# Dilated attention of a two-block network: strided values projected feature-major, scores over 64 partitions in two banks

## The chip, the cores and the metric

The kernel runs on one core of one Trainium2 chip. The metric is device time in microseconds (us) of one launch, the median of several runs. A profiled execution is one more launch, of which the hardware profiler kept every instruction; all rows below are from such an execution.

## The reference, cut to what matters

Two network blocks on 1024 tokens of 1024 features follow each other. The second block normalises its input, projects it with one matrix and feeds four mixers, of which dilated attention is one. It has twelve heads of 64 features in three groups of four. A group has a window and a dilation (128 and 1, 512 and 4, 2048 and 16). The tokens of a group are taken apart by the dilation, and each query attends to the keys of its own and the previous band:

```
def dilated_group(q, k, v, bias_tab, window, dil):
    ...
    qb = to_sub(q).reshape(B_, dil, H, nb, band, E)
    kb = band_keys(to_sub(k))
    vb = band_keys(to_sub(v))
    ...
    s = jnp.einsum('bdhnqe,bdhnke->bdhnqk', qb, kb, preferred_element_type=jnp.float32) / math.sqrt(E)
    s = jnp.where(mask[None, None, None], s + bias[None, None, :, None], -1e30)
    m = jnp.max(s, axis=-1, keepdims=True)
    p = jnp.exp(s - m)
    den = jnp.sum(p, axis=-1, keepdims=True)
    o = jnp.einsum('bdhnqk,bdhnke->bdhnqe', p, vb.astype(jnp.float32)) / den
    lse = (m + jnp.log(den))[..., 0]
    ...
```

The three groups' outputs are then weighted by a softmax over their `lse`.

## The kernel before

`build` runs the first block, then `stick`, `dilated`, `s5` (with the pooling mixer) and the merge of the second block. Everything is written by hand against one core; a scheduler sets the order of each engine's instructions at build time, and that order is then fixed. Activations lie feature-major: eight tiles of 128 features by 1024 tokens, each in a high and a low f32r part (`xh`, `xl`), so that a product is three products (high by high, low by high, high by low).

`gemm` (L357, L359, L361) makes a feature-major projection: 128 output features, 8 feature tiles, two halves of 512 tokens, three products, so 48 matmuls with 512 moving columns, where a weight tile is stationary. Its weights come through `load_w` (L325), which loads 512 KB and splits it on ACT (L381) and DVE (L382). `tm_gemm` (L1581 to L1583) makes a token-major projection instead: 128 tokens of x are stationary, 256 columns of weights move, 24 matmuls for a block of 128 tokens.

`dilated` goes through three groups g with dilations 1, 4 and 8 (the third group's 16 is handled as 8 with every second distance masked). For each group:

- a bias tile per head (L1733), made from a small table;
- values V (L1743 to L1752): 8 blocks of 128 tokens by `tm_gemm`, where `nat` picks each block's tokens, so that for g of 1 and 2 the stationary operand is every 4th or 8th column of x; ACT copies each result to `vd` (L1751);
- queries and keys by `gemm`, m from 0 to 3: ACT writes q (`dq`, L1761), with the tokens put into strided order on the way; each k is written twice into tiles of 128 partitions that POOL has set to zero (`dk`, L1767), head 0 of a pair by DVE into partitions 0 to 63 (L1772), head 1 by ACT into 64 to 127 (L1770), so that a product over 128 partitions takes one head alone;
- 8 blocks n of 128 queries: scores of the four heads (L1790), with 128 or 256 keys, two heads of a pair side by side in one PSUM bank; bias and maximum on DVE (L1793), exponential on ACT (L1798), transposes on TensorE (L1803), copies `dpt` to SBUF (L1806, L1808), products with V (L1815), copies of the result to `num` (L1818, L1820).

Ahead of group 0's blocks and behind every second block `fill` puts one gate projection of the later merge (`gate`, another `gemm` of 48 matmuls), which the scheduler lays between the block's own steps. At the end the groups are weighted: two more gates, then 24 products over 32 partitions (L1883). Two PSUM places of 1024 columns (`pmm`, tiles `mm`) and four banks (`pax`, tiles `ax`) are shared by all of this.

Of the kernel before, what the change touches and what calls it, by code (L numbers as in the profile page):

```python
# [30 lines left out]
# pieces of the down-projection, those by plain products, and when a piece's parts are made:  # L31
# counted in products before the next piece, and around those of a pair of rows
# [7 lines left out]
# ---------------------------------------------------------------- host layout  # L40
# [98 lines left out]
def layout(i):  # L139
# [58 lines left out]
    A["w_dv"] = np.stack([np.ascontiguousarray(wd[:, 2, g]).reshape(KC, P, 256) for g in range(3)])  # L198
# [53 lines left out]
# ---------------------------------------------------------------- device code  # L252


class Kern:
# [26 lines left out]
    # two places, in turn unless the caller says which  # L282
# [15 lines left out]
    # one gate of the merge, to keep the tensor engine busy meanwhile  # L298
# [25 lines left out]
    # weights of one output tile, split into two f32r parts  # L324
# [11 lines left out]
    # up to four weight tiles, split  # L336
# [11 lines left out]
    # out[128 features, tokens] for each (psum AP, list of hi APs, list of lo APs)  # L348
# [14 lines left out]
    # activations are lists of feature tiles for each half of the tokens  # L363
# [6 lines left out]
    # slots that hold two feature tiles of one half  # L370
# [17 lines left out]
    # y = v^-1/2 for a small tile v, by Newton steps from an integer guess  # L388
# [15 lines left out]
    # running sum of (g x)^2 over the feature tiles  # L404
# [9 lines left out]
    # sums over partitions, token-major [128, blocks]  # L414
# [8 lines left out]
    # token-major [128, blocks] to a row that all partitions hold  # L423
# [23 lines left out]
    # rows r1 = rstd(x) and r1 * rstd(x r1 g), from the sums of x^2 and (g x)^2  # L447
# [15 lines left out]
    # (x * rstd) * g + s, split  # L463
# [18 lines left out]
    # ------------------------------------------------------------ adaptive modulation  # L482
# [21 lines left out]
    # ------------------------------------------------------------ first block, mixing half  # L504
    def block1_mix(self):
# [18 lines left out]
        # the stages of a normed tile: times rstd, scaled, shifted, split  # L524
# [104 lines left out]
        # output gates, queries of both mixers  # L629
# [37 lines left out]
        # the context  # L667
# [50 lines left out]
        # token-major projections: values and gates  # L718
# [37 lines left out]
        # keys and queries of the recurrent heads, the other modulation columns in between  # L756
# [27 lines left out]
        # the last recurrent head comes last  # L784
# [10 lines left out]
        # output projection onto the residual, with the norm that follows  # L795
# [12 lines left out]
    # last products of a residual, a half of the tokens at a time, each half's norm under the next products;  # L808
    # the residual goes to DRAM, the normed activations B become the seven right factors of the
    # 2 x 2 product of Strassen and Winograd (rows: halves of the features, columns: halves of the tokens)  # L810
# [30 lines left out]
    # T1 = B12 - B11, T3 = B22 - B12, T2 = T3 + B11, -T4 = B21 - T2, the last three in the place of x  # L841
# [37 lines left out]
    # one row of the up-projection's tiles a and v, by seven products instead of eight:  # L879
    # a = A11 B1 + A12 B2, v = A21 B1 + A22 B2 over the halves of the features  # L880
# [49 lines left out]
    # gated hidden units to DRAM; the first two pairs side by side while the factors are formed  # L930
    def up(self, fp, W, B, steps, act):
# [11 lines left out]
        for j in range(2, NF):  # L943
            # the last product of a pair behind the first one of the next
            new = run(j)
            next(new)
            next(cur)
            for _ in range(5):
                next(new)
            cur = new  # L950
# [3 lines left out]
    # hidden units back on chip in pieces, times the down-projection onto the residual, by seven  # L954
    # products over the halves of features and tokens; the last piece is left to the caller,
    # for the norm that follows
    def down(self, fp, W, xd, yd, add):
# [5 lines left out]
        # the right factors of a piece, in the order of the products  # L963
# [53 lines left out]
        # both parts of the first and the last piece  # L1017
# [17 lines left out]
        # rows m and m + 4 of the output: what is done when, counted in products  # L1035
        def pair(m, j0, pn, B):
# [21 lines left out]
            # S3 in the place of A11, S4 in that of A21  # L1058
# [68 lines left out]
    # recurrent heads and window attention side by side  # L1127
# [13 lines left out]
    def window(self, ep, qd, kd, kcd, va):  # L1141
        nc, A = self.nc, self.A
        ID = self.c("ident")
        # keys of a group twice along the partitions, for queries that hold both parts of their split
# [14 lines left out]
        # the queries of a unit, high parts over low parts  # L1159
# [17 lines left out]
        # shifted exponentials of the scores, over their sum  # L1177
# [40 lines left out]
        def values(n, v, ss, rd):  # L1218
# [22 lines left out]
            if v:  # L1241
                # over the sums of the exponentials, as rows
# [23 lines left out]
    # depthwise convolution of three taps along the tokens of a PSUM tile  # L1266
# [6 lines left out]
    def mlstm(self, ep, km, kc, qm, vx, so, G):  # L1273
# [6 lines left out]
        # log sigmoid of the forget gates  # L1280
# [37 lines left out]
        # in token order, and token-major copies  # L1318
# [26 lines left out]
        for h in range(4):  # L1345
# [4 lines left out]
            # states at the chunk starts  # L1350
# [46 lines left out]
            # decay from key to query and from the chunk start to the query  # L1397
# [34 lines left out]
            # outputs of both directions  # L1432
# [30 lines left out]
            # norm over the head's features, gain and output gate  # L1463
# [20 lines left out]
    # ------------------------------------------------------------ first block, feed-forward half  # L1484
# [30 lines left out]
    # ------------------------------------------------------------ second block  # L1515
    # both norms between the blocks, under the last products of the first block
    def block2_norm(self, xs, out):
# [14 lines left out]
        # queries and keys of the first head, first half of the tokens  # L1532
# [30 lines left out]
    # token-major projection of 128-token blocks: out[tokens, columns]  # L1563
# [26 lines left out]
    # ------------------------------------------------------------ stick-breaking attention  # L1590
    def stick(self):
# [36 lines left out]
        with tc.tile_pool(name="sb", bufs=1) as fp:  # L1628
# [54 lines left out]
            for h in range(4):  # L1683
# [3 lines left out]
                # the next head's projections, or a gate, between the two halves of the queries  # L1687
# [13 lines left out]
    # ------------------------------------------------------------ dilated attention  # L1701
    def dilated(self):
# [3 lines left out]
        with tc.tile_pool(name="dl", bufs=1) as fp:  # L1706
# [10 lines left out]
            for g, dil in enumerate((1, 4, 8)):  # L1717
                # additive bias and mask of each head, Toeplitz in query and key
# [24 lines left out]
                wh, wl = self.tm_weights(A["w_dv"][g], 256)  # L1743
                vs = []
                for b in range(8):
                    if b % 4 == 0:
                        vt = self.big("vd")
                    ps = self.pax(256)
                    self.tm_gemm(ps, lambda x: nat(x, b), wh, wl)
                    v = vt[:, (b % 4) * 256 : (b % 4 + 1) * 256]  # L1750
                    nc.scalar.activation(v, ps, AF.Copy)  # L1751
                    vs.append(v)  # L1752
                q, k = [], []
                for m in range(4):
# [3 lines left out]
                    pv = ps.rearrange("p (l s) -> p l s", s=dil)  # L1758
                    if m < 2:
                        t = self.big("dq")  # L1760
                        nc.scalar.activation(t.rearrange("p (s l) -> p l s", s=dil), pv, AF.Copy, scale=0.125)  # L1761
                        q.append(t)
                    else:
                        kk = []
# [598 lines left out]
```

## Time and profile before

| | |
|---|---|
| three runs | 3555.98, 3558.32, 3559.59 us; median 3558.32 |
| span of the profiled execution, first to last instruction | 3555.0 us |
| TensorE matmul (PE) busy | 3405.7 us, 96% |
| VectorE (DVE) busy | 2235.6 us, 63% |
| ScalarE (ACT) busy | 1288.1 us, 36% |
| GpSimd (POOL) busy | 895.6 us, 25% |
| mean granted clock of TensorE | 0.988 of full speed |

The profile gives the span only; what a run takes beyond the span is the difference of the first two lines, 3.3 us at the median. A matmul's duration in the rows reaches from its start to its modelled end, and matmuls overlap, so the pace of a sequence is read from the distance of starts. `dilated` lies between 1683 and 2200 us of the span.

### The profile page before, as it was taken

What the parts mean: (1) busy time and instruction counts of PE and PEld (TensorE: products, weight loads), DVE (VectorE), ACT (ScalarE), POOL (GpSimd) and SP (SyncE); (2) the same over time, 40 slices, a digit from 0 to 9 for tenths busy, and PEclk for the clock granted to TensorE, in tenths of its full rate; (3) what the DMA queues carried; (4) which work ended last, traced back from release to release, by engine and by line L of the source; (5) the groups of instructions that cost most, each with busy time, mean ns of one, the idle gap of its engine ahead of it and who ended that gap; (6) DMA issues with size and microseconds to landing.
All of it is one profiled execution on the core that took longest, in us unless ns stands there. A gap on an engine that the chain in (4) does not pass through costs nothing. (4 is left out here: it accounts for less than half of the span.)

```text
span 3555.0 us, 43191 instructions
## 1 busy us (share of the span) xinstructions
PE 3405.7 (96%) x15923; PEld 2710.8 (76%) x15923; DVE 2235.6 (63%) x4029; ACT 1288.1 (36%) x2424; POOL 895.6 (25%) x654
## 2 busy tenths in 40 slices
PE   6999998989999999999999999999999989999998
PEld 4797765868888777777878888877778768888777
DVE  8746776697877897577121215646456685555796
ACT  5224555443333334355232233122222343333332
POOL 3200000065655542100000000231023055454440
PEclk9999999999999999999999999999999999999999
DMA  6555111512221422201221103122374522223332
GB/s 234 187 160 166 37 57 51 169 66 89 77 83 66 166 92 81 89 30 36 67 61 34 63 30 112 54 97 69 110 257 145 166 83 81 86 78 121 98 94 79
DMA packets 141490, 348.63 MB, mean 98 GB/s; under 512 B 16712, under 2 KB 43744, under 8 KB 141280
## 3 DMA queue, kind: packets, MB, share of 16 engines
q1 hardware_dynamic: 141280, 345.88, 28.9%
q8 instruction: 125, 2.05, 0.2%
q14 instruction: 85, 0.70, 0.1%
HBM read 270.67 MB, written 75.16 MB: 97 GB/s over the span
## 5 line engine op out<-in xcount | busy, mean ns | idle before, releaser
L381 ACT ACTIVATE wh<-w 128x512 fp32r<-128x512 f32 (+1 forms) x500 | 303.2, 610 | 1006.5 <-PE mm L359 629.3
L382 DVE TENSOR_TENSOR wl<-w,wh 128x512 fp32r<-128x512 f32 (+1 forms) x500 | 365.9, 736 | 479.6 <-ACT wh L381 458.9
L361 PE MATMUL ax<-bh,wl 128*128 128x512 f32 x928 | 369.6, 399 | 15.3 <-DVE wl L382 15.2
L359 PE MATMUL ax<-bl,wh 128*128 128x512 f32 x928 | 370.4, 399 | 5.9 <-DVE bl L382 5.7
L357 PE MATMUL ax<-bh,wh 128*128 128x512 f32 x928 | 368.4, 398 | 4.7 <-ACT bh L381 4.7
L357 PE MATMUL mm<-bh,wh 128*128 128x512 f32 x864 | 327.8, 401 | 16.1 <-DVE x L2304 6.3
L361 PE MATMUL mm<-bh,wl 128*128 128x512 f32 x864 | 321.2, 396 | 3.8 <-DVE wl L382 3.6
L359 PE MATMUL mm<-bl,wh 128*128 128x512 f32 x864 | 322.5, 394 | 0.0
L357 PE MATMUL mm<-xh,wh 128*128 128x512 f32 x880 | 289.3, 404 | 2.3 <-DVE sql L385 1.8
L361 PE MATMUL mm<-xh,wl 128*128 128x512 f32 x880 | 289.4, 403 | 0.0
L359 PE MATMUL mm<-xl,wh 128*128 128x512 f32 x880 | 288.0, 403 | 0.0
L382 DVE TENSOR_TENSOR wl<-ws,wh 128x512 fp32r<-128x512 f32 x176 | 216.3, 1238 | 31.6 <-ACT wh L381 31.4
L891 POOL TENSOR_TENSOR ws<-w 128x512 f32<-128x512 f32 x44 | 84.6, 1922 | 578.7 <-DMA w<-in_w_up_dram 508.3
L361 PEld LDWEIGHTS ax<-bh,wl 128*128 128x128 f32 x928 | 177.0, 191 | 59.8 <-DVE wl L382 19.4
L357 PEld LDWEIGHTS mm<-bh,wh 128*128 128x128 f32 x864 | 162.5, 188 | 71.7 <-DVE x L2304 11.6
L359 PEld LDWEIGHTS ax<-bl,wh 128*128 128x128 f32 x928 | 176.4, 190 | 51.2 <-DVE bl L382 10.1
L357 PEld LDWEIGHTS ax<-bh,wh 128*128 128x128 f32 x928 | 176.2, 190 | 46.7 <-ACT bh L381 6.1
L361 PEld LDWEIGHTS mm<-bh,wl 128*128 128x128 f32 x864 | 162.5, 188 | 45.3 <-DVE wl L382 7.1
L357 PEld LDWEIGHTS mm<-xh,wh 128*128 128x128 f32 x880 | 162.3, 189 | 42.3 <-issue 5.3
L359 PEld LDWEIGHTS mm<-xl,wh 128*128 128x128 f32 x880 | 165.1, 189 | 38.3 <-issue 2.8
L361 PEld LDWEIGHTS mm<-xh,wl 128*128 128x128 f32 x880 | 164.2, 188 | 37.6 <-issue 2.0
L359 PEld LDWEIGHTS mm<-bl,wh 128*128 128x128 f32 x864 | 162.9, 189 | 35.2
(632 smaller groups left out, 7437.3 us busy)
## 6 DMA issues: line engine op xcount, KB each, us to landing
w<-in_w_up_dram SPq DMA_DIRECT2D x88, 512.0 KB
wa<-in_w_ada_dram SPq DMA_DIRECT2D x64, 512.0 KB
w<-in_w_out_dram SPq DMA_DIRECT2D x32, 512.0 KB
w<-in_w_gate_dram SPq DMA_DIRECT2D x32, 512.0 KB
gd<-gf SPq DMA_DIRECT2D x32, 512.0 KB
g<-gd SPq DMA_DIRECT2D x32, 512.0 KB
y<-y SPq DMA_DIRECT2D x28, 512.0 KB
w<-in_w_down_dram SPq DMA_DIRECT2D x24, 512.0 KB
```

The costliest lines, as they stand in the source:

```text
L357: nc.tensor.matmul(ps, lhsT=wh, rhs=xh[k], start=s, stop=False, **kw)
L359: nc.tensor.matmul(ps, lhsT=wh, rhs=xl[k], start=False, stop=False, **kw)
L361: nc.tensor.matmul(ps, lhsT=wl, rhs=xh[k], start=False, stop=e, **kw)
L381: first = nc.scalar.activation(hi, src, AF.Copy)
L382: nc.vector.tensor_tensor(lo, src, hi.bitcast(F32), ALU.subtract)
L891: nc.gpsimd.tensor_tensor(t, x, y, op)
```

## The change

For g of 1 and 2 the values are made feature-major, by two more `gemm` projections whose results ACT writes in strided order into `dvf` tiles; `turn` then turns each of these with 8 TensorE transposes into the token-major `vd` tiles, copied by DVE. Group 0 keeps `tm_gemm`. Of q and k, m of 0 and 2 are written by ACT and m of 1 and 3 by DVE, whole, each once; the zeroed key tiles are gone. The scores of a head are products over its own 64 partitions; the two heads of a pair go to two PSUM banks, head r of both pairs into bank r.

```
-    A["w_dv"] = np.stack([np.ascontiguousarray(wd[:, 2, g]).reshape(KC, P, 256) for g in range(3)])
+    A["w_dv0"] = np.ascontiguousarray(wd[:, 2, 0]).reshape(KC, P, 256)
+    A["w_dvf"] = np.concatenate([fm(np.ascontiguousarray(wd[:, 2, g])) for g in (1, 2)], 0)
...
-                wh, wl = self.tm_weights(A["w_dv"][g], 256)
-                vs = []
-                for b in range(8):
-                    if b % 4 == 0:
-                        vt = self.big("vd")
-                    ps = self.pax(256)
-                    self.tm_gemm(ps, lambda x: nat(x, b), wh, wl)
-                    v = vt[:, (b % 4) * 256 : (b % 4 + 1) * 256]
-                    nc.scalar.activation(v, ps, AF.Copy)
-                    vs.append(v)
+                vt = [self.big("vd") for _ in range(2)]
+                vs = [vt[b // 4][:, (b % 4) * 256 : (b % 4 + 1) * 256] for b in range(8)]
+                vf = []
+                if g == 0:
+                    wh, wl = self.tm_weights(A["w_dv0"], 256)
+                    for b in range(8):
+                        ps = self.pax(256)
+                        self.tm_gemm(ps, lambda x: nat(x, b), wh, wl)
+                        nc.scalar.activation(vs[b], ps, AF.Copy)
+                else:
+                    for m in range(2):
+                        hi, lo = self.load_w(A["w_dvf"][2 * (g - 1) + m], D)
+                        ps = self.pmm()
+                        self.gemm(hi, lo, self.xtargets(ps, self.xh2, self.xl2))
+                        t = self.big("dvf")
+                        nc.scalar.activation(t.rearrange("p (s l) -> p l s", s=dil), ps.rearrange("p (l s) -> p l s", s=dil), AF.Copy)
+                        vf.append(t)
+                def turn(m):
+                    for i in range(2):
+                        pp = self.pax()
+                        for b in range(4):
+                            c = (4 * i + b) * P
+                            nc.tensor.transpose(pp[:, b * P : (b + 1) * P], vf[m][:, c : c + P], ID)
+                        o = vt[i].rearrange("p (b c) -> p b c", b=4)[:, :, m * P : (m + 1) * P]
+                        nc.vector.tensor_copy(o, pp.rearrange("p (b c) -> p b c", b=4))
...
-                    if m < 2:
-                        t = self.big("dq")
-                        nc.scalar.activation(t.rearrange("p (s l) -> p l s", s=dil), pv, AF.Copy, scale=0.125)
-                        q.append(t)
+                    t = self.big("dq" if m < 2 else "dk")
+                    if m % 2:
+                        nc.vector.tensor_scalar(t.rearrange("p (s l) -> p l s", s=dil), pv, 0.125 if m < 2 else 1.0, None, ALU.mult)
                     else:
-                        kk = []
-                        for r in range(2):
-                            t = self.big("dk")
-                            nc.gpsimd.memset(t, 0.0)
...
+                        nc.scalar.activation(t.rearrange("p (s l) -> p l s", s=dil), pv, AF.Copy, scale=0.125 if m < 2 else 1.0)
+                    (q if m < 2 else k).append(t)
+                    if vf and m in (1, 2):
+                        turn(m - 1)
...
+                    pr = [self.pax(), self.pax()]
                     for j in range(2):
-                        ps = self.pax()
-                        for r in range(2):
-                            o = ps[:, r * 256 : r * 256 + W]
-                            nc.tensor.matmul(o, lhsT=q[j][:, sl], rhs=k[j][r][:, k0 : (n + 1) * P], start=True, stop=True)
                         for r in range(2):
...
+                            hp = slice(64 * r, 64 * r + 64)
+                            nc.tensor.matmul(pr[r][:, j * 256 : j * 256 + W], lhsT=q[j][hp, sl], rhs=k[j][hp, k0 : (n + 1) * P], start=True, stop=True)
+                    for h in range(4):
+                        j, r = divmod(h, 2)
+                        nc.vector.tensor_tensor_reduce(
+                            s4[:, h, c0:256], pr[r][:, j * 256 : j * 256 + W], bias[h][:, c0:256], 1.0, -3e38, ALU.add, ALU.max, m4[:, h : h + 1]
+                        )
```

Since instructions move, their order on TensorE stands here at three places of group 1. Names are tiles with running numbers; the changed file has its lines 1 further on up to the values and 13 further on in the blocks (L361 is L362, L1790 is L1803, L1803 is L1816).

TensorE, the start of group 1's values, before: behind the last bias product (`hk`) come 192 matmuls with strided tokens stationary.

```order
L1733 MATMUL ax_15190<-hk_15188,const 128x256
L1581 MATMUL ax_15207<-wth_15196,xh_11268 128x256
L1582 MATMUL ax_15207<-wtl_15197,xh_11268 128x256
L1583 MATMUL ax_15207<-wth_15196,xl_11276 128x256
L1581 MATMUL ax_15207<-wth_15196,xh_11269 128x256
```

The same place in the change:

```order
L1734 MATMUL ax_15182<-hk_15180,const 128x256
L360 MATMUL mm_15198<-xl_11283,wh_15194 128x512 x2
L362 MATMUL mm_15198<-xh_11275,wl_15195 128x512 x2
L358 MATMUL mm_15259<-xh_11268,wh_15251 128x512 x2
L360 MATMUL mm_15259<-xl_11276,wh_15251 128x512 x2
```

The first value projection (`mm_15198`) already stands around the bias products, where the first query projection stood; the second (`mm_15259`) follows, and then queries and keys.

TensorE in the change, behind the second query projection (`mm_15381`): the 8 transposes of the first value tile.

```order
L360 MATMUL mm_15381<-xl_11283,wh_15377 128x512 x2
L362 MATMUL mm_15381<-xh_11275,wl_15378 128x512 x2
L1768 MATMUL ax_15432<-const,dvf_15247 128x128 x4
L1768 MATMUL ax_15438<-const,dvf_15247 128x128 x4
L358 MATMUL mm_15454<-xh_11268,wh_15446 128x512 x2
L360 MATMUL mm_15454<-xl_11276,wh_15446 128x512 x2
```

They stand in a row between two projections, one projection after the value tile was complete; the second value tile's 8 follow the first key projection in the same way.

TensorE, the first scores of group 1, before: `dk` and `dq` are keys and queries, `mm_15754` is a gate.

```order
L1790 MATMUL ax_15672<-dk_15597,dq_15475 128x128
L1790 MATMUL ax_15672<-dk_15600,dq_15475 128x128
L357 MATMUL mm_15754<-xh_11268,wh_15746 128x512 x2
L359 MATMUL mm_15754<-xl_11276,wh_15746 128x512 x2
L361 MATMUL mm_15754<-xh_11268,wl_15747 128x512
L1790 MATMUL ax_15677<-dk_15662,dq_15536 128x128
L361 MATMUL mm_15754<-xh_11268,wl_15747 128x512
L357 MATMUL mm_15754<-xh_11269,wh_15746 128x512 x2
L1790 MATMUL ax_15677<-dk_15665,dq_15536 128x128
```

In the change:

```order
L1803 MATMUL ax_15582<-dk_15503,dq_15369 128x128
L1803 MATMUL ax_15583<-dk_15503,dq_15369 128x128
L358 MATMUL mm_15664<-xh_11268,wh_15656 128x512 x2
L360 MATMUL mm_15664<-xl_11276,wh_15656 128x512 x2
L362 MATMUL mm_15664<-xh_11268,wl_15657 128x512
L1803 MATMUL ax_15582<-dk_15576,dq_15430 128x128
L1803 MATMUL ax_15583<-dk_15576,dq_15430 128x128
L362 MATMUL mm_15664<-xh_11268,wl_15657 128x512
```

The second pair's two scores now stand together behind 5 matmuls of the gate, since both wait for one copy of the key tile instead of two; the two heads of a pair go to two banks.

## Rows read from the trace of the kernel before

**Rows 1.** The page, part 1: busy time of each engine.

```profile
PE 3405.7 (96%) x15923; PEld 2710.8 (76%) x15923; DVE 2235.6 (63%) x4029; ACT 1288.1 (36%) x2424; POOL 895.6 (25%) x654
```

**Rows 2.** Busy time by stretch of the span; the sum is over the three block loops.

```profile
core 0: us, PE busy (x) PEld busy (x) DVE busy (x) ACT busy (x) POOL busy (x), PEclk, DMA share, GB/s
...
1710.00:1722.00 12.00, 12.00 (x103) 12.00 (x103) 0.00 (x0) 1.54 (x4) 0.00 (x0) 1.00 0.00 1
...
2070.00:2097.00 27.00, 27.00 (x118) 21.85 (x117) 5.27 (x6) 6.77 (x7) 0.00 (x0) 1.00 0.12 39
...
2184.00:2200.00 16.00, 15.36 (x43) 9.87 (x42) 16.00 (x19) 3.14 (x3) 1.27 (x1) 0.68 0.44 133
2200.00:2400.00 200.00, 199.55 (x956) 165.71 (x955) 116.54 (x379) 49.06 (x95) 51.55 (x62) 1.00 0.26 87
...
sum 224.00, PE 221.26 PEld 167.41 DVE 76.82 ACT 101.94 POOL 6.48; mean PE 73.75 PEld 55.80 DVE 25.61 ACT 33.98 POOL 2.16
```

**Rows 3.** Timeline of TensorE: first row of each strided value projection, first behind it.

```profile
1852.38 0.48 PE L1581 MATMUL ax<-wth,xh 128*128 128x256 f32 x1
...
1897.48 0.63 PE L359 MATMUL mm<-xl,wh 128*128 128x512 f32 x2
...
2022.11 0.49 PE L1581 MATMUL ax<-wth,xh 128*128 128x256 f32 x1
...
2068.53 0.63 PE L357 MATMUL mm<-xh,wh 128*128 128x512 f32 x2
```

**Rows 4.** Timeline of TensorE in group 1: transposes (L1803) and value products (L1815) among gates.

```profile
1953.78 0.63 PE L357 MATMUL mm<-xh,wh 128*128 128x512 f32 x2
1954.35 0.33 PE L1803 MATMUL ax<-const,ds 128*128 128x128 f32 x1
1954.43 0.47 PE L359 MATMUL mm<-xl,wh 128*128 128x512 f32 x1
1954.74 0.32 PE L1803 MATMUL ax<-const,ds 128*128 128x128 f32 x1
...
1963.58 0.63 PE L357 MATMUL mm<-xh,wh 128*128 128x512 f32 x2
```

**Rows 5.** Timeline of TensorE: scores of two blocks, value products, first row behind each.

```profile
1762.32 1.05 PE L1790 MATMUL ax<-dk,dq 128*128 128x128 f32 x8
1763.13 0.71 PE L357 MATMUL mm<-xh,wh 128*128 128x512 f32 x2
...
1957.45 1.99 PE L1790 MATMUL ax<-dk,dq 128*128 128x256 f32 x8
1959.09 0.81 PE L361 MATMUL mm<-xh,wl 128*128 128x512 f32 x2
...
1964.14 1.14 PE L1815 MATMUL ax<-dpt,vd 128*64 128x128 f32 x16
1965.22 0.73 PE L359 MATMUL mm<-xl,wh 128*128 128x512 f32 x2
```

**Rows 6.** Copies out of PSUM, by tile (ns: least/median/most).

```profile
L1772 DVE COPY dk<-mm x6: 1217/1954/1997, 1740.3 to 2098.0; 64x1024 f32<-64x1024 f32 x6
...
L1761 ACT ACTIVATE dq<-mm x6: 1007/1996/2017, 1727.7 to 2075.8; 128x1024 f32<-128x1024 f32 x6
...
L1808 DVE COPY dpt<-ax x11: 691/692/693, 1775.7 to 1998.1; 128x512 f32<-128x512 f32 x11
```

**Rows 7.** Groups of TensorE by shape, 1683 to 2240 us.

```profile
L1790 PE MATMUL ax<-dk,dq 128*128 128x256 f32 x88 | 21.6, 388 | 0.0
L1790 PE MATMUL ax<-dk,dq 128*128 128x128 f32 x104 | 15.2, 282 | 2.7 <-ACT dk L1770 1.7 <-DVE dk L1772 1.0
```

**Rows 8.** Waits of TensorE, 1683 to 2260 us (total us, times, longest).

```profile
PE ax L1790 <- ACT dk L1770: 1.7, 2, 0.9
PE ax L1790 <- DVE dk L1772: 1.0, 2, 0.5
```

More of the change, by code (lines that the diff above doesn't have):

```diff
@@ L1758, in dilated @@
                     pv = ps.rearrange("p (l s) -> p l s", s=dil)
-                    if m < 2:
-                        t = self.big("dq")
-                        nc.scalar.activation(t.rearrange("p (s l) -> p l s", s=dil), pv, AF.Copy, scale=0.125)
-                        q.append(t)
-                    else:
-                        kk = []
-                        for r in range(2):
-                            t = self.big("dk")
-                            nc.gpsimd.memset(t, 0.0)
-                            sl = slice(64 * r, 64 * r + 64)
-                            if r:
-                                nc.scalar.activation(t.rearrange("p (s l) -> p l s", s=dil)[sl], pv[sl], AF.Copy)
-                            else:
-                                nc.vector.tensor_copy(t.rearrange("p (s l) -> p l s", s=dil)[sl], pv[sl])
-                            kk.append(t)
-                        k.append(kk)
+                    t = self.big("dq" if m < 2 else "dk")
+                    if m % 2:
+                        nc.vector.tensor_scalar(t.rearrange("p (s l) -> p l s", s=dil), pv, 0.125 if m < 2 else 1.0, None, ALU.mult)
+                    else:
+                        nc.scalar.activation(t.rearrange("p (s l) -> p l s", s=dil), pv, AF.Copy, scale=0.125 if m < 2 else 1.0)
+                    (q if m < 2 else k).append(t)
+                    if vf and m in (1, 2):
+                        turn(m - 1)
                 nt = [self.big("num") for _ in range(2)]
@@ L1785, in dilated @@
                     nm = self.small(4, "nm")
+                    pr = [self.pax(), self.pax()]
                     for j in range(2):
-                        ps = self.pax()
                         for r in range(2):
-                            o = ps[:, r * 256 : r * 256 + W]
-                            nc.tensor.matmul(o, lhsT=q[j][:, sl], rhs=k[j][r][:, k0 : (n + 1) * P], start=True, stop=True)
-                        for r in range(2):
-                            h = 2 * j + r
-                            nc.vector.tensor_tensor_reduce(
-                                s4[:, h, c0:256], ps[:, r * 256 : r * 256 + W], bias[h][:, c0:256], 1.0, -3e38, ALU.add, ALU.max, m4[:, h : h + 1]
-                            )
+                            hp = slice(64 * r, 64 * r + 64)
[5 more added lines that the diff above has]
+                        )
                     nc.vector.tensor_scalar(nm, m4, -1.0, None, ALU.mult)
```

## The prediction

> **What bounds the kernel.** The page comes first: TensorE is busy for 96% of the span, VectorE for 63% [rows 1]. A whole-span share says little about one stage, so the stretches come next. In the three block loops of the dilated attention TensorE is busy for 221.26 of 224 us, while DVE has 76.82 and ACT 101.94 us of work [rows 2]. In a stretch of projections alone it is busy for 27.00 of 27 us, and in the 200 us that follow the stage for 199.55 [rows 2]. In this stage TensorE is thus the bound, before and behind the change's places too: what its own instructions lose in time comes off the span, and what DVE, ACT and POOL do costs nothing unless TensorE comes to wait for it. A busy share does not say that TensorE runs at its best pace, though, so I then read the distance of starts in the timeline.
>
> There lies the fault that the change attacks. Group 0's values, with consecutive tokens stationary, run 103 matmuls in 12.00 us [rows 2], 0.117 us each. The same instruction in groups 1 and 2 takes far longer: 192 matmuls fill 1852.38 to 1897.48, 45.10 us or 0.235 each, and 2022.11 to 2068.53, 46.42 us or 0.242 each [rows 3]. In group 0 such a value projection has 256 moving columns just the same; only the stride of the stationary tokens differs. A projection with 512 moving columns takes 27.00 us for the 118 matmuls that touch the stretch [rows 2], some 116 whole ones, 0.2325 us each. A strided token-major matmul thus costs what one of twice the columns costs.
>
> **The change, part by part.**
>
> *Values of groups 1 and 2.* Removed: 45.10 + 46.42 = 91.52 us of TensorE [rows 3]. Added: two projections a group, 4 x 48 = 192 matmuls at 0.2325 = 44.64 us. Gain 46.9 us.
>
> *Turning them back.* 4 x 8 = 32 transposes of 128 by 128. A lone transpose among gates takes, with one gate matmul, 1954.35 to 1954.74 [rows 4], so 0.39 - 0.23 = 0.16 us. A score pass of the same shape, eight in a row, takes 0.81 / 8 = 0.10 us [rows 5]. Here eight stand in a row, but each is fresh work for the array; I take 0.13, halfway: cost 4.2 us, bounds 3.2 and 5.1. The four DVE copies a group are like the `dpt` copy of 0.69 us [rows 6]; they and the strided copies of the value tiles on ACT, like those of q at 2.0 us [rows 6], are covered by projections of 11 us each, in which TensorE waits for none of them. By the order in front, each value tile has a whole projection's time before it is turned and more before it is used. If that cover were gone, a turn's copies would cost some 1.4 us each time.
>
> *Scores.* 96 score matmuls appear as 88 + 104 passes [rows 7], two passes each. The four scores of a block with 256 keys take 1957.45 to 1959.09 = 1.64 us, with 128 keys 1762.32 to 1763.13 = 0.81 us [rows 5]. There are 88 / 8 = 11 blocks of the first kind and 104 / 8 = 13 of the second. The number of passes and their columns stay; a pass uses half of the array's rows, and the two heads of a pair lie in different halves and banks, so they may run beside each other. No row of this trace shows two row halves at work. The nearest are the value products, which write halves of the output partitions: 16 passes of 128 columns in 1964.14 to 1965.22 = 1.08 us [rows 5], 0.0675 each where a full pass took 0.10, two thirds. I take two thirds of 1.64 us for the long blocks, a gain of 11 x 0.54 = 6.0 us, and nothing for the short ones, where a pass of 0.10 us holds a load of 128 columns too, which stays; the value products load 64. Lower bound of the cost: both kinds halve, 11 x 0.82 + 13 x 0.40 = 14.3 us gained. Upper bound: nothing overlaps and each of the 24 blocks pays 0.1 us more to enter and to leave the smaller tile, 4.8 us lost; 0.1 us is what entering the value products costs, 1963.58 to 1964.14 where two gate matmuls take 0.465 [rows 4, 5].
>
> On that entry: transposes, which keep the whole array, are entered at the same cost, 1953.78 to 1954.35 [rows 4], so the 0.1 us here comes with any product that waits for another engine, and I add none for the tile in the sum. [...]
>
> *Key tiles.* Twelve memsets of POOL go, and nothing of TensorE waited for them. Before, a pair's keys were written by DVE in up to 2.0 us [rows 6] and then by ACT, and TensorE waited 1.7 + 1.0 = 2.7 us in all [rows 8]. Now one copy of 2.0 us stands between the last projection and the second pair's scores, with 5 gate matmuls (1.16 us) and two scores (0.3) in front; some 0.7 us of waiting stay in each of two groups. Gain 1.3 us. Behind that DVE copy in its queue stand a weight split and the first reductions, which need the scores anyway.
>
> *Loads.* Weights move the same bytes (two 512 KB tiles a group instead of two of 512 KB), now needed 11 us apart. The stretch of projections shows that such a pace is held without a gap [rows 2].
>
> **Sum.** -46.9 + 4.2 - 6.0 - 1.3 = -50.0 us. The profiled span of 3555.0 becomes 3505.0; the median of the runs shown is 3.3 us above that span, so 3558.3 becomes **3508.3**, 1.4% less. A measurement of this kernel can tell about 0.2%, 7 us, from no change.
>
> **The rivals.**
>
> 1. *The row halves don't overlap.* For it: the value products show an overlap of output halves only, and of two passes of one score the second must follow the first. Against it: the halves share neither rows nor a bank. Then the scores gain nothing, or lose up to 4.8 us: 3514 to 3519.
>
> 2. *They overlap wholly*, the load of one half passing under the product of the other: 14.3 us instead of 6.0, 3500. Against it: passes of 128 columns at 0.10 us look bound by their loads. [...]
>
> 3. *The gain stays under another chain.* If DVE's weighting of the groups or the next mixer's start set its own time, part of 50 us would come back as a wait. Half of it gives 3533. Against it: DVE and ACT are at a third to under a half of the block loops, and TensorE has 0.45 us of gaps in the 200 us behind [rows 2].
>
> 4. *Slower: the clock falls in the block loops.* Around the products over 32 partitions the mean granted clock is 0.68 in 2184 to 2200, between its two levels, and TensorE does 43 matmuls in 15.36 busy us, 0.357 each where projections take 0.2325 [rows 2]. If products over 64 partitions did the same, matmul work in the 224 us of loops would cost 0.357 / 0.2325 - 1 = 54% more, up to 120 us: 3628. It decides from 93 us of such work, where 50 us are used up. Against it: these products last at most 1.64 us between full-array projections, whereas those over 32 partitions, with waits between, fill most of that stretch of 16 us.
>
> 5. *It doesn't do what it says*: the new projections run slower than others, because ACT's strided copies hold a PSUM place. Against it: query projections with the same 2.0 us copies run on at full pace [rows 2, 6]. No gain at all would need 46.9 us of new waits; 3555.
>
> **How the numbers follow.** My forecast (3503 to 3513) has a chance of 0.50, rival 1 0.25, rival 2 0.14, rival 3 0.05, rival 4 0.03, rival 5 0.03. The range takes in forecast, rivals 1 and 2 and the bounds of the transposes (1 us each way) and of a run against another (2 us): 3497 to 3522. It leaves out rivals 3 to 5, 0.11. Faster by over 0.2%: 0.50 + 0.25 + 0.14 + 0.05 = 0.94; within: 0.03; slower: 0.03.
>
> **What would show it.** In the profile after, the rows of the strided value projections are gone, and four more projections of 11.2 us stand in their place; the block loops' stretches of scores with 256 keys last about 1.1 us where they lasted 1.64, those with 128 keys about 0.8; eight transposes last about 1 us; TensorE's waits for the keys fall to some 1.4 us in all; its gaps in the stage stay below 6 us and its clock at 1.00 in the loops. I am wrong on the scores if the long blocks take 1.6 us or 0.8, on the bound if new waits of TensorE for ACT, DVE or loads of over 5 us appear, and on the whole if the span falls by less than 36 or more than 61 us.

## The result, and the profile after

The changed kernel takes **3505.7 us** (median of 4 runs, 3502.9 to 3506.9) where the kernel before takes 3558.1 (4 runs): a ratio of 0.9848, 95% interval 0.9836 to 0.9860. That is 52.4 us less; forecast were 50.0 less, 3508, in 3497 to 3522. The profiled execution has a span of 3505.2 us, 49.8 less than before.

The busy times of the page answer to [rows 1]:

```profile
PE 3355.7 (96%) x15763; PEld 2644.2 (75%) x15763; DVE 2239.1 (64%) x4041; ACT 1280.0 (37%) x2410; POOL 883.7 (25%) x642
```

TensorE lost 50.0 us of busy time and kept its share; DVE, ACT and POOL changed by at most 12 us. The stretches of the three block loops and 200 us behind the stage answer to [rows 2] (columns: window, length, TensorE busy and instructions, granted clock, DMA share, GB/s):

```profile
1763.09:1838.00 74.91, 74.91 (x452) 1.00 0.19 61
1906.93:1979.00 72.07, 71.78 (x419) 1.00 0.19 59
2047.57:2113.00 65.43, 65.12 (x368) 1.00 0.20 60
2148.00:2348.00 200.00, 199.56 (x955) 1.00 0.26 86
```

TensorE has 0.6 us of gaps in the loops, at a clock of 1.00, and as few behind the stage as before. No other engine took over as the bound.

Where the time went is read from landmarks in TensorE's timeline. "After, again" is a second profiled execution of the changed kernel, on another chip.

| from, to (us) | before | after | after, again |
|---|---|---|---|
| start to the first scores of group 0 | 1762.32 | 1763.09 | 1761.81 |
| to the first scores of group 1 | 169.56 | 143.84 | 143.83 |
| to the first scores of group 2 | 165.90 | 140.64 | 140.44 |
| to the first product of the merge | 87.14 | 84.98 | 84.97 |
| to the end of the span | 1370.08 | 1372.65 | 1370.15 |

The two middle steps and the next give 25.7 + 25.3 + 2.2 = 53.1 us. The 2.6 us that this profile shows as given back behind the stage are scatter of one execution: the second has 1370.15 there, as before, and over all profiles kept for this document, whose work is the same there, that stretch takes 1367.9 to 1372.7.

A turn of a value tile, with the row ahead of it and the first row behind it (timeline of TensorE, group 1: start, us, line, output and inputs, shapes, count):

```profile
1882.77 1.03 PE L1768 MATMUL ax<-const,dvf 128*128 128x128 f32 x8
1883.56 0.70 PE L358 MATMUL mm<-xh,wh 128*128 128x512 f32 x2
...
1894.34 0.64 PE L362 MATMUL mm<-xh,wl 128*128 128x512 f32 x2
1894.81 1.04 PE L1768 MATMUL ax<-const,dvf 128*128 128x128 f32 x8
1895.61 0.71 PE L358 MATMUL mm<-xh,wh 128*128 128x512 f32 x2
```

Eight transposes take 1883.56 - 1882.77 = 0.79 us (four times in all, 3.2 us), and the projection between two turns 1894.81 - 1883.56 = 11.25. The scores of a block with 128 keys and of one with 256 answer to [rows 5]:

```profile
1762.53 0.63 PE L362 MATMUL mm<-xh,wl 128*128 128x512 f32 x2
1763.09 0.71 PE L1803 MATMUL ax<-dk,dq 64*128 64x128 f32 x8
1763.73 0.74 PE L358 MATMUL mm<-xh,wh 128*128 128x512 f32 x2
...
1769.06 1.13 PE L1803 MATMUL ax<-dk,dq 64*128 64x256 f32 x8
1770.12 0.50 PE L362 MATMUL mm<-xh,wl 128*128 128x512 f32 x1
```

The short block takes 0.64 us (0.81 before), the long one 1.06 (1.64 before). Before, a block's time hung on what stood ahead of it: long ones took 1.54 us behind gate products and 1.64 behind value products, short ones 0.81 and 0.91 (1780.38 to 1781.92 and 2121.21 to 2122.12 are such blocks). [rows 5] sets a long block behind value products beside a short one behind gates. In the change the row ahead makes no such difference: long blocks take 1.06 to 1.07 us and short ones 0.64 to 0.65, behind either. The row ahead of the short block starts 0.56 us before it; before, the same two gate products took 0.45 to 0.47. TensorE's waits for the keys, which were 2.7 us in all [rows 8], are now (line, what for; total us, times, longest):

```profile
PE ax L1803 <- DVE dk L1781: 0.6, 2, 0.3
```

### The profile page after: what moved, and what is told of

Its sections match the earlier page's. It is cut to its first block, busy times and chain, and to the rows that moved or that the text cites. A ratio compares the mean times of both kernels' runs of the same rounds, so it can differ in the third digit from the quotient of the medians.

```text
span 3505.2 us, 42846 instructions
## 1 busy us (share of the span) xinstructions
PE 3355.7 (96%) x15763; PEld 2644.2 (75%) x15763; DVE 2239.1 (64%) x4041; ACT 1280.0 (37%) x2410; POOL 883.7 (25%) x642
## 4 chain that ended last, share of the span: by engine, by line
PE 80%; DVE 12%; issue 2%; DMA 2%; ACT 2%; POOL 1%; SPq 0%; DVEq 0%; ACTq 0%; POOLq 0%
PE mm L358 15%; PE mm L360 15%; PE mm L362 15%; PE ax L362 6%; PE ax L360 6%; PE ax L358 6%; DVE bl L383 2%; PE ax L1236 2%; PE ax L1649 1%; DVE wl L383 1%; PE ax L1582 1%; PE ax L1584 1%; PE ax L1583 1%; PE mm L1649 1%; PE ax L1229 1%
## 5 line engine op out<-in xcount | busy, mean ns | idle before, releaser
L362 PE MATMUL ax<-bh,wl 128*128 128x512 f32 x928 | 369.9, 400 | 15.2 <-DVE wl L383 15.1
L362 PE MATMUL mm<-bh,wl 128*128 128x512 f32 x864 | 321.0, 396 | 3.8 <-DVE wl L383 3.6
L358 PE MATMUL mm<-xh,wh 128*128 128x512 f32 x944 | 311.1, 404 | 2.3 <-DVE sql L386 1.8
L362 PE MATMUL mm<-xh,wl 128*128 128x512 f32 x944 | 312.6, 403 | 0.0
L360 PE MATMUL mm<-xl,wh 128*128 128x512 f32 x944 | 305.0, 401 | 0.0
L362 PEld LDWEIGHTS ax<-bh,wl 128*128 128x128 f32 x928 | 176.9, 191 | 59.7 <-DVE wl L383 19.0
L362 PEld LDWEIGHTS mm<-xh,wl 128*128 128x128 f32 x944 | 176.4, 188 | 44.5 <-issue 5.8
L358 PEld LDWEIGHTS mm<-xh,wh 128*128 128x128 f32 x944 | 174.3, 188 | 46.3 <-issue 6.3
L360 PEld LDWEIGHTS mm<-xl,wh 128*128 128x128 f32 x944 | 177.9, 189 | 40.9 <-issue 1.5
L362 PEld LDWEIGHTS mm<-bh,wl 128*128 128x128 f32 x864 | 162.6, 188 | 45.5 <-DVE wl L383 7.0
```

The lines of the kernel that those rows point to most:

```text
L358: nc.tensor.matmul(ps, lhsT=wh, rhs=xh[k], start=s, stop=False, **kw)
L360: nc.tensor.matmul(ps, lhsT=wh, rhs=xl[k], start=False, stop=False, **kw)
L362: nc.tensor.matmul(ps, lhsT=wl, rhs=xh[k], start=False, stop=e, **kw)
```

## The experiments

"The stage" below is the time from the first matmul of group 0's value projection to the start of the last row of products of the merge, in the profiled execution: 490.1 us before, 437.1 after. Ratios are to the kernel before on the same chip.

**One part at a time.** e1_values puts the new `vt`, `vf` and `turn` of the change into the kernel before:

```
+        hi, lo = self.load_w(A["w_dvf"][2 * (g - 1) + m], D)
+        self.gemm(hi, lo, self.xtargets(ps, self.xh2, self.xl2))
...
+        turn(m - 1)
```

> The kernel before with the values' part alone: feature-major projections of the strided groups' values, copies and turns; scores and keys as before. Theory (the strided tokens as stationary operand cost the time): the value sections lose 91.5 us and gain 44.6 + 4 x 0.79 = 47.8, so 3558 - 43.7 = 3514 us (3511 to 3517), eight turns in 0.79 us, long score blocks still 1.64 us. Rival (a good part of the gain needs the other part too, by slots or PSUM places that only come free with it): above 3522.

Measured: 3515.0 us, ratio 0.9870 (0.9855 to 0.9885); expected were 3514 of 3558, 0.988. The turns take 0.79 us and the long score blocks 1.64. e2_scores is the rest of the change: values as before, scores and keys new.

```
+        hp = slice(64 * r, 64 * r + 64)
+        nc.tensor.matmul(pr[r][...], lhsT=q[j][hp, sl], rhs=k[j][hp, ...])
```

> The kernel before with the part of the scores and keys alone; values token-major with strided tokens as before. Theory (row halves run beside each other): long blocks 1.06 us where 1.64, short ones 0.65 where 0.81, entry from a full-array product 0.56 where 0.47, key waits 0.6 us where 2.7: 3558 - 6.1 - 2.2 + 1.1 - 2.1 = 3549 us (3546 to 3552). Rival (the blocks are shorter but TensorE then waits for the reductions or the copies): 3556 to 3560.

Measured: 3550.6 us, ratio 0.9967 (0.9953 to 0.9981); expected were 3549 of 3558, 0.9975. Long blocks take 1.06 us, short ones 0.65. TensorE's waits for the keys in e1_values, then in e2_scores:

```profile
PE ax L1812 <- ACT dk L1790: 1.7, 2, 0.9
...
PE ax L1812 <- DVE dk L1792: 1.0, 2, 0.5
```

```profile
PE ax L1781 <- DVE dk L1761: 0.6, 2, 0.3
```

The stage is 43.5 us shorter in the one and 11.2 in the other, 54.7 together, and 53.0 with both. The two parts add up to within 1.7 us, and neither needs the other. Of the 1.7 us, 0.8 are waits of the bias products in groups 1 and 2 for their tables' transfers (0.5 us in either part, 1.3 with both); what makes the rest is not shown.

**Is it the stride?** e3_consecutive changes only the tokens that the kernel before holds stationary in groups 1 and 2:

```
-        self.tm_gemm(ps, lambda x: nat(x, b), wh, wl)
+        self.tm_gemm(ps, lambda x: x[:, b * P : (b + 1) * P], wh, wl)
```

> The kernel before, in which the values of groups 1 and 2 are projected from consecutive tokens, as those of group 0; it leaves out the stride, so that the values of these groups stand in another order than their scores. Theory (the stride of the stationary operand costs the time): 2 x 192 matmuls at 0.117 us take 22.4 us a group where 45.1 and 46.4, 3558 - 46.7 = 3511 us (3508 to 3514). Rival (the token-major form itself in this place: its ACT copies, its PSUM places or its weights): the group keeps some 45 us, 3558.

Measured: 3512.1 us, ratio 0.9864 (0.9847 to 0.9880); the values of each group take 22.8 us. The token-major form costs nothing in itself; the stride does (45.10 and 46.42 us at strides of 4 and 8). Then the stride alone is varied, to 2 and to 3:

```
+        self.tm_gemm(ps, lambda x: nat(x, b) if g == 0 else x[:, (b // 2) * 256 + b % 2 : (b // 2) * 256 + 256 : 2], wh, wl)
...
+        self.tm_gemm(ps, lambda x: nat(x, b) if g == 0 else x[:, b * 64 : b * 64 + 382 : 3], wh, wl)
```

> The kernel before, in which the values of groups 1 and 2 are projected from every second token; it leaves out the strides of 4 and 8, so that the values stand in another order than their scores. Three theories of the price of a stride: any stride costs the same (4 and 8 cost the same, 0.235 and 0.242): 3558 us; the price rises with the stride and is full at 4: about half, some 34 us a group, 3535; a stride of 2 is free: 3511. I hold the first likeliest.

> The kernel before, in which the values of groups 1 and 2 are projected from every third token; it leaves out the strides of 4 and 8. A load of 128 columns took 188 ns at stride 1, 196 at stride 2, 335 at strides 4 and 8. If the price comes with strides above 2 at once: 335 ns and some 45 us a group. If it comes with the power of two, or with 4: near 196 ns and 23 us a group. If it rises between: some 265 ns and 34 us.

Measured: stride 2 takes 3516.3 us (ratio 0.9874, 0.9857 to 0.9891) and 23.3 and 23.2 us a group; stride 3 takes 3536.4 in one run, and 33.7 and 33.6 us a group. What I held likeliest for stride 2 was wrong: it is nearly free. The groups of weight loads of these products, at strides 1, 2 and 3, and then in the kernel before at strides 4 (group 1) and 8 (group 2) (partitions x columns, count; busy us, mean ns):

```profile
L1581 PEld LDWEIGHTS ax<-wth,xh 128*128 128x128 f32 x128 | 24.0, 188 | 0.1
```

```profile
L1581 PEld LDWEIGHTS ax<-wth,xh 128*128 128x128 f32 x128 | 25.1, 196 | 0.1
```

```profile
L1581 PEld LDWEIGHTS ax<-wth,xh 128*128 128x128 f32 x128 | 33.5, 262 | 0.1
```

```profile
L1581 PEld LDWEIGHTS ax<-wth,xh 128*128 128x128 f32 x64 | 21.2, 331 | 0.0
...
L1581 PEld LDWEIGHTS ax<-wth,xh 128*128 128x128 f32 x64 | 21.6, 338 | 0.0
```

So the load's price is nearly nothing at a stride of 2 fp32 values, half paid at 3, and nearly full at 4: 188, 196, 262, 331 and 338 ns. A matmul, its 256 moving columns the same, then costs 22.8 / 192 = 0.119, 0.121, 0.175, 0.235 and 0.242 us. These loads overlap each other, since each lasts longer than one matmul's pace (188 ns to 119, 331 to 235), so a load's length is not itself the pace; but the pace rises with it, which I read as the load having become what sets it. At a stride of four a matmul took twice as long as at one (0.235 us for 0.119). Why a stride makes the load longer is not shown.

**Halves of the rows, banks, order.** e6_full_rows keeps the change's banks and order and takes the row halves away:

```
-        lhsT=q[j][hp, sl], rhs=k[j][hp, k0 : (n + 1) * P]
+        lhsT=q[j][:, sl], rhs=k[j][:, k0 : (n + 1) * P]
```

> The changed kernel with scores over all 128 partitions in its two banks and its order; it leaves out the parting of the two heads of a pair, so that each score is the sum of two. Theory (row halves give the gain): blocks of 1.64 and 0.81 us again and entry at 0.47, + 6.1 + 2.2 - 1.1 = + 7.2 us, 3513. Rival (the two banks give it): 1.06 and 0.65 stay, 3505.7.

Measured: 3512.2 us, ratio 0.9867 (0.9852 to 0.9881); the stage is 6.0 us longer than with the change. A long block and the first row behind it:

```profile
1951.66 1.99 PE L1803 MATMUL ax<-dk,dq 128*128 128x256 f32 x8
1953.31 0.82 PE L362 MATMUL mm<-xh,wl 128*128 128x512 f32 x2
```

1.65 us again: the gain is the row halves', not the banks'. Whether the halves would gain as much with one bank for both was not tried. The run also parts the new keys from the row halves, since it has the one and not the other. From a group's first scores to the start of its last row of value products (us):

| | group 0 | group 1 | group 2 | sum |
|---|---|---|---|---|
| before | 71.05 | 67.19 | 59.63 | 197.87 |
| e6_full_rows | 70.60 | 66.32 | 58.79 | 195.71 |
| after | 67.12 | 63.55 | 57.71 | 188.38 |

The last rows of value products of group 0, before and after, with the first scores at 1762.32 and 1763.09:

```profile
1833.37 1.15 PE L1815 MATMUL ax<-dpt,vd 128*64 128x128 f32 x16
...
1830.21 1.15 PE L1828 MATMUL ax<-dpt,vd 128*64 128x128 f32 x16
```

In these loops the new keys, with the two banks, are thus worth 2.2 us (TensorE waits 0.9 for keys in e6_full_rows) and the row halves 7.3. That the stage differs by 6.0 only comes from between the loops, where the change takes 1.4 us more, 0.8 of it the waits for the bias tables. e5_halves_apart asks how the halves give it, by the order of the four products:

```
-        for j in range(2):
-            for r in range(2):
+        for r in range(2):
+            for j in range(2):
```

> The changed kernel with the four scores of a block in another order: both heads of the upper rows first, then both of the lower rows. Theory of steps (a product's two passes follow each other, and a product in the other row half may start beside the last pass of the one before it): A B A B takes 5 steps of 0.21 us = 1.06, A A B B takes 7 = 1.49 us for 256 keys; for 128 keys some 0.78 where 0.65; 11 x 0.43 + 13 x 0.13 = 6.4 us more, 3512 us. Rival (a pass over half of the rows is itself shorter, order or not): 1.06 and 0.65 stay, 3505.7.

Measured: 3514.7 us, ratio 0.9871 (0.9856 to 0.9886), but the blocks stay at 1.07 and 0.65. The time came from elsewhere: TensorE waits for exponentials (`ds`), which it does not in the change.

```profile
PE ax L1816 <- ACT ds L1811: 4.5, 12, 0.4
```

The first exponential of a long block in the change, whose scores start at 1798.07, and in this run, where they start at 1801.46, with the transpose that waits here:

```profile
1800.99 0.51 ACT L1811 ACTIVATE ds<-ds,nm 128x256 f32<-128x256 f32 x1 [1.74 <-DVE nm L1809]
...
1804.39 0.51 ACT L1811 ACTIVATE ds<-ds,nm 128x256 f32<-128x256 f32 x1 [1.75 <-DVE nm L1809]
1805.04 0.44 PE L1816 MATMUL ax<-const,ds 128*128 128x128 f32 x2 [0.40 <-ACT ds L1811]
```

The exponential begins 2.92 and 2.93 us behind the scores, so it is not later here. But with the new order the scheduler laid 8 gate matmuls between a long block's scores and its first transpose, where the change has 10 to 12, and TensorE comes there too early. The stage is 4.7 us longer. My theory of steps, which put long blocks at 1.49, fell. Taken alone, this run speaks for the rival, that a pass over 64 rows is shorter by itself. e10_same_half puts that to the test with no second half to run in:

```
-        hp = slice(64 * r, 64 * r + 64)
+        hp = slice(0, 64)
```

> The changed kernel with all four scores of a block over the upper 64 partitions, so that no two can lie in different row halves; it leaves out the lower heads' scores, which repeat the upper ones. If the row halves run beside each other, whatever their order: eight passes in a row, 1.64 and 0.81 us. If a pass over 64 rows is shorter by itself: 1.06 and 0.65 us as before.

Measured: 3518.7 us in one run. A short block and a long one, with the rows behind:

```profile
1765.08 1.16 PE L1803 MATMUL ax<-dk,dq 64*128 64x128 f32 x8
1766.16 0.50 PE L358 MATMUL mm<-xh,wh 128*128 128x512 f32 x1
```

```profile
1771.36 1.99 PE L1803 MATMUL ax<-dk,dq 64*128 64x256 f32 x8
1773.28 0.50 PE L362 MATMUL mm<-xh,wl 128*128 128x512 f32 x1
```

1.08 and 1.92 us: longer than over the whole array, so a pass over 64 rows is not shorter. The halves do run beside each other, and that in either order. How many of a block's eight passes have begun by a given moment shows it; each window begins before the block and ends later than the window above it (columns as in the stretches). The change:

```profile
1779.70:1780.10 0.40, 0.23 (x2) 1.00 0.00 0
1779.70:1780.25 0.55, 0.39 (x4) 1.00 0.00 0
1779.70:1780.50 0.80, 0.64 (x6) 1.00 0.00 0
1779.70:1780.70 1.00, 0.83 (x8) 1.00 0.00 0
```

e5_halves_apart, in windows that end as long after its block's start, and e10_same_half, likewise:

```profile
1782.20:1782.60 0.40, 0.24 (x2) 1.00 0.00 0
...
1782.20:1783.20 1.00, 0.84 (x8) 1.00 0.00 0
```

```profile
1782.86:1783.26 0.40, 0.24 (x1) 1.00 0.00 0
1782.86:1783.41 0.55, 0.39 (x2) 1.00 0.00 0
1782.86:1783.66 0.80, 0.64 (x3) 1.00 0.00 0
1782.86:1783.86 1.00, 0.84 (x4) 1.00 0.00 0
```

With two halves, passes start in pairs; with one half, singly, at the same pace. What the row tiles cost is read between blocks that all stand behind gates, and from a block's start to the start of the second row behind it, when the gates are back at their pace; two gate matmuls, 0.465 us, lie between. Shown are that second row for the block with 128 keys that starts at 1762.32 before, at 1763.09 in the change and at 1765.08 in e10_same_half, then a block with 256 keys and its second row. The kernel before:

```profile
1763.68 0.63 PE L359 MATMUL mm<-xl,wh 128*128 128x512 f32 x2
...
1780.38 1.89 PE L1790 MATMUL ax<-dk,dq 128*128 128x256 f32 x8
...
1782.56 0.63 PE L359 MATMUL mm<-xl,wh 128*128 128x512 f32 x2
```

The change, then e10_same_half:

```profile
1764.31 0.62 PE L360 MATMUL mm<-xl,wh 128*128 128x512 f32 x2
...
1779.87 1.14 PE L1803 MATMUL ax<-dk,dq 64*128 64x256 f32 x8
...
1781.49 0.62 PE L360 MATMUL mm<-xl,wh 128*128 128x512 f32 x2
```

```profile
1766.74 0.62 PE L360 MATMUL mm<-xl,wh 128*128 128x512 f32 x2
...
1783.02 1.99 PE L1803 MATMUL ax<-dk,dq 64*128 64x256 f32 x8
...
1785.52 0.62 PE L360 MATMUL mm<-xl,wh 128*128 128x512 f32 x2
```

With 256 and with 128 keys that is 2.18 and 1.36 us over the whole array, 1.62 and 1.22 with two halves, 2.50 and 1.66 with one. From 128 to 256 keys, a pass grows by (2.18 - 1.36) / 8 = 0.103 us over the whole array, by (2.50 - 1.66) / 8 = 0.105 in one half, and a pair by (1.62 - 1.22) / 4 = 0.10: a pair costs what one pass costs. Taking pass or pair as proportional to its columns, a long block has 16, 16 and 8 such pieces. Less these and the two gate matmuls, 2.18 - 1.64 - 0.47 = 0.07 is left over for the whole array, 2.50 - 1.68 - 0.47 = 0.35 for one half, 1.62 - 0.80 - 0.47 = 0.35 for two. By this estimate row tiles cost some 0.28 us more a block, and 0.09 ahead of it where a gate stands there; overlap pays for that. Behind value products the whole array pays 0.1 itself, and the difference is some 0.18. The runs thus show that the two halves overlap (0.10 us for a pair of passes, 0.103 for one pass) and, by this estimate, that each such block has a fixed price; what that price is made of they do not show.

**Versions that might beat both.** e7_transfer projects all values from consecutive tokens and lets DMA put them in order, without turns:

```
+        self.tm_gemm(ps, lambda x: x[:, b * P : (b + 1) * P], wh, wl)
...
+        nc.sync.dma_start(VD[i * 512 : (i + 1) * 512, :].rearrange("(b p) c -> p b c", p=P), ...)
+        nc.sync.dma_start(vs[b], bass.AP(VD.tensor, VD.offset + s0 * 256, [[dil * 256, P], [1, 256]]))
```

> The changed kernel with the values of groups 1 and 2 projected token-major from consecutive tokens, as in group 0, written to DRAM and read back in the strided order by eight transfers a group; no turns and no copies of them. Theory (DMA queues have room, and 45 us of projections cover the way): 192 matmuls at 0.117 = 22.4 us a group as with two projections, and the turns (4 x 0.79 = 3.2 us) are gone: 3502.5 us. Rival (the transfers stand before the weights in SP's queue, or come late for the first value products): 3507 or more.

Measured: 3508.4 us, ratio 0.9854 (0.9839 to 0.9869). The stage is 433.6 us, 3.5 less than with the change, about the 3.2 us of the turns, though 0.8 of it are shorter waits for the bias tables; the time does not tell it from the change. e8_alternate takes the two heads of a pair in turn in the value products:

```
-        for h in range(4):
...
-            for i, t in enumerate(pt):
+        for j in range(2):
+            for h, i in [(2 * j + r, i) for i in range(len(pt)) for r in range(2)]:
```

> The changed kernel with the value products of a block in another order: the two heads of a pair, which write different partitions, in turn for each part of the keys, instead of both parts of one head and then of the other. By the theory of steps more passes pair up: a block of 16 passes falls from 1.07 us towards 9 x 0.107 = 0.96; 11 such blocks give 1.2 us, 3504.5, to be read from the rows and not from the time. Rival (column halves don't overlap in that way, or the loads set the pace): 1.07 stays.

Measured: 3505.1 us, ratio 0.9842 (0.9826 to 0.9858). A block of 16 passes and the row behind it:

```profile
1782.84 1.09 PE L1829 MATMUL ax<-dpt,vd 128*64 128x128 f32 x16
1783.86 0.50 PE L362 MATMUL mm<-xh,wl 128*128 128x512 f32 x1
```

1.02 us where 1.07, not 0.96: 11 x 0.05 = 0.6 us. The stage is 1.7 us shorter, but 0.8 of it are waits for the bias tables' transfers in the two later groups (0.5 us here, 1.3 and 1.1 in the two profiles of the change); no run shows what moves them. e9_both joins the two edits, with the change beside it:

> The changed kernel with the transfers of e7_transfer and the order of the value products of e8_alternate together. From the first bias product to the last product of the merge the stage was 3.5 us shorter in the one and 1.7 us in the other. If the two add up: 5.2 us less than the changed kernel, which is timed beside it, near 3500.5 where that has 3505.7. Rival (the time saved comes back as waits behind the stage): within 2 us of the changed kernel.

> The changed kernel itself once more, as the mark for e9_both on the same chip: 3505.7 us, 0.985 of the kernel before, whatever theory holds.

Measured: 3502.8 us, ratio 0.9841 (0.9827 to 0.9855), beside 3507.3, 0.9848 (0.9835 to 0.9861). The stage is 433.1 us beside 437.0, 3.9 less and not the 5.2 hoped for, with 0.4 of it from the bias tables. 4.4 us of median lie within the intervals: likely a gain of 0.1%, not shown by the time.

## Why the prediction was right, and where not

**The bound held.** TensorE's own instructions set the time in the stage, and what they lost came off the span. e1_values and e2_scores add up to within 1.7 us, which fits a stage where no other engine takes over.

**Values: right in cause and size.** Forecast were 46.9 us gained and 4.2 given back by the turns, 42.7 net. From the last row of value products of one group to the first scores of the next the section fell from 98.51 to 76.72 and from 98.71 to 77.09 us, 43.4 together; e1_values alone shortens the stage by 43.5. The projections came as costed; the turns took 0.79 us each, 3.2 in all, the lower bound, because eight transposes in a row run at the pace of the score passes (0.79 / 8 = 0.099 us each, 0.81 / 8 = 0.10 for those). That the stride is the cause was read from group 0 and argued; e3_consecutive shows it.

**Scores: near in size, in part by luck, and wrong in reason.** Forecast were 6.0 us: two thirds for the long blocks, nothing for the short, nothing for the tile's entry. Between e6_full_rows and the change the row halves are worth 7.3 us. The step "a load of 128 columns, which stays" failed: the short blocks fell from 0.81 us behind gates and 0.91 behind value products to 0.65. The step "I add none for the tile" failed too. The row on which it stood, transposes entered at 0.57, does not speak for row tiles: the 12 blocks behind gates are entered 0.09 us later than before, and each block keeps some 0.28 more inside behind gates, some 0.18 behind value products. The overlap of rival 2 is what happens: the halves overlap wholly, in either order (0.10 us for a pair of passes where one pass takes 0.103; long blocks of 1.06 us in the change and 1.07 in e5_halves_apart); that one half's load passes under the other's product was not shown. A price for each block, the 0.28 and 0.18 us, is also there, and the entry behind gates. By the estimates above, overlap is worth 11 x 0.82 + 13 x 0.40 = 14.2 us, the row tiles cost 12 x 0.37 + 12 x 0.18 = 6.6, and 7.6 remain, against 7.3 measured: a large gain and a large cost, neither in the sum, that happened to leave something near 6.0. The two prices that the forecast started from, 1.64 and 0.81, were also not alike, one read behind value products and the other behind gates. Two thirds came near because the row it came from, the value products over half the columns, is a tiled block of two overlapping halves itself. Its passes, in the changed kernel's block that starts at 1786.23, begin in pairs too:

```profile
1786.10:1786.35 0.25, 0.12 (x2) 1.00 0.00 0
1786.10:1786.45 0.35, 0.22 (x4) 1.00 0.00 0
```

So its 0.0675 us a pass was no evidence of a partial overlap.

**Key waits: right in kind.** 2.7 us fell to 0.6, a gain of 2.1 where 1.3 was forecast; by the loops of e6_full_rows the new keys are worth 2.2. I had priced the rest at 0.7 us in each of two groups; it is 0.3.

**The sum.** 43.4 + 7.3 + 2.2 and 0.2 behind the last value products make the 53.1 of the landmarks, against 52.4 between the medians and 50.0 forecast. The misses: values 0.7 (the turns 1.0 cheaper), scores 1.3, keys 0.9, all toward less time.

**The rivals.** Rival 1 (no overlap) fell with e10_same_half. Rival 3 (another chain) fell: behind the stage TensorE has 0.44 us of gaps in 200, as before. Rival 4 (the clock) fell: 1.00 in all three loops. Rival 5 fell with the projections of 11.25 us.

## What to carry to other kernels

Price a stationary operand by its stride: fp32 at a stride of 2 was nearly free here (a load of 196 ns for 188), and at 4 and 8 the load took 331 and 338 ns and a 256-column matmul twice the time, 0.235 and 0.242 us for 0.119, so compare the start-to-start times of one instruction at two places before believing a busy share. Two heads in two row halves run side by side (a pair of passes took 0.10 us, as one pass did), but by the estimate above each such block cost some 0.2 to 0.4 us more than one over the whole array, so it may pay to pack more products into one block, which no run tried. And when one order is changed, look at what moves with it: e5_halves_apart left the products as fast as they were, but the transposes came two to four gate matmuls earlier, and 4.5 us of waits for exponentials appeared.

## What the runs showed that was not expected

- The price of a stride is graded: 188, 196, 262 and 331 ns for loads at strides of 1, 2, 3 and 4 fp32 values, and hardly more, 338, at 8.
- Products in the two row halves pair up even where both of one half are issued first: 1.07 us and pairs of passes in e5_halves_apart. Since passes of one half begin singly (in e10_same_half, 1, 2, 3 and 4 have begun where two halves have 2, 4, 6 and 8), a product issued third must have begun before the two ahead of it were done.
- Four products in one row half took 1.92 us where the whole array takes 1.64: a small tile without a partner was slower than zero padding.
- What stands ahead of a block has a price: scores over the whole array took 0.1 us longer behind value products than behind gates (1.64 and 1.54 us, 0.91 and 0.81).
